# Seven-product feed-forward network of a hybrid backbone: who rounds, who empties PSUM, and in what order TensorE takes its products

## The chip, the cores and the metric

The kernel runs on one core of a Trainium2 chip. The metric is the device time of one execution in microseconds (us). TensorE is called PE here, VectorE DVE, ScalarE ACT, GpSimd POOL, and the queue that issues most transfers SP.

## The reference, cut to what matters

Two layers, each on 1024 latent tokens and 256 context tokens of width 1024. In front of each half of a layer stands a normalisation that is modulated by six vectors, which come from a small input times a large matrix (the "modulations", 1024 x 6144 a layer).

```
m = silu(c) @ w_mod[l] + b_mod[l]          # sh1, sc1, ga1, sh2, sc2, ga2; the same for c_ctx
x = x + ga1 * (mixers(modulate(rms_norm(x), sh1, sc1) @ w_in) @ w_out)
x = x + ga2 * (square(relu(modulate(rms_norm(x), sh2, sc2) @ w_ffn1)) @ w_ffn2)
```

w_ffn1 is 1024 x 4096, w_ffn2 4096 x 1024. The context tokens go through the same with their own modulations, in the last layer only as far as the mixers need them. All is fp32.

## The kernel before, in words

**Products.** An fp32 factor is split in two: a rounded part h (fp32r) and the rest l = x - h. Each product is three matmuls, h·h, h·l and l·h (`mm3`, L141 to L143). So every weight passes one rounding copy and one subtraction on POOL: `split` (L243), in which ACT does the copy (`copy_a`, L130) and POOL the subtraction (L246). `wcols` loads a block of 128 columns of w_ffn1 in two halves of 256 KB through two `raw` buffers (L258); the parts `wh` and `wl` have three buffers each.

**The first layer of the feed-forward network** multiplies the hidden rows (two groups of 512 latent tokens) by w_ffn1 with seven block products instead of eight. The first of the seven, and the whole of the context tokens, are the *first sweep*, `hidden_first` (L1249): for each block `fc` of 128 columns it sums over k = 0 to 7. For the latent rows (even `fc` alone; layer 1 has only these) it copies PSUM after k = 3, while the sum goes on in the same bank:

```
if k == 3 and t0 >= CTX:
    r = self.B()
    self.copy_a(r, ps)
    self.nc.scalar.dma_start(self.part[fc // 2], r)
```

The half sum is kept in HBM (`part`). At the end `squared` (L1243) empties PSUM with a relu, squares and stores, all on ACT. The other six products are the *second sweep*, `hidden_rest` (L1271), in 16 rounds. A round loads a 1024 x 256 block (`weights`, L1283), makes the four sums of its quarters on DVE (L1300 to L1303), rounds five of them on ACT and subtracts on POOL (L1306, L1309), and does the products in `front` and `m5`, `c21`, `c12`, `m7`.

**The quarter** (L1203) makes the other factor's eight combinations for the second sweep from the last group of rows. For four k it has two normalised rows each (a DVE instruction with PSUM, then a bias added by ACT, L133), five DVE additions (L1229 to L1234), and six POOL subtractions (L1230, L1240), five of them each after a rounding copy on ACT.

**Modulations.** A bank (`mod_bank`, L306) multiplies 2048 columns of w_mod by two columns of the input, in 32 columns of PE for each of four groups of PE's columns: 8 steps of k, in each two loads of 512 KB and four fp32 products, two after each load. A product shows as two matmul records. The tiles come from `land`: for the two banks woven into a layer these are the three `e` buffers, for the others `u`.

**Order.** `weave` interleaves generators by their share of a written cost. That gives the priority in which instructions are laid out. The framework's planner then places them on the engines' queues by its own costs, a ready one ahead of one that waits. On the chip each queue is fixed and goes strictly in order. The first sweep is woven with the end of the normalisation and the quarter (`ffn`, L1367); the banks 1 and 2 of the modulations with projections; bank 0 of layer 1 with the last product of layer 0.

Of the kernel before, what the change touches and what calls it, by code (L numbers as in the profile page):

```python
# [13 lines left out]
P = 128  # L14
# [79 lines left out]
class Net:  # L94
# [148 lines left out]
    def split(self, h, l, raw):  # L243

        self.copy_a(h, raw)
        self.nc.gpsimd.tensor_sub(l, raw, f(h))  # L246

# [57 lines left out]
    def mod_bank(self, l, b, land, tag="po"):  # L305
# [3 lines left out]
        for k in range(KD):  # L309
            for hf in range(2):  # L310
# [3 lines left out]
                for q in range(2):  # L314
                    cg = 2 * hf + q
                    nc.tensor.matmul(ps[32 * cg:32 * cg + 32, :], self.csil[:, 2 * k:2 * k + 32], raw[:, 512 * q:512 * q + 512],  # L316
                                     start=k == 0, stop=k == KD - 1, skip_group_check=True,
                                     tile_position=(0, 32 * cg))
                yield 0.9
# [884 lines left out]
    def quarter(self, h, t, x, l, t0, rs):  # L1204
# [12 lines left out]
        def row(k):  # L1217
            a = self.S(n)
            self.stt(a, x.at(k, t0, n), p["s"][1][:, k, 0:1], rb, ALU.mult, ALU.mult)
            self.act(a, a, AF.Identity, bias=p["mods"][:, 24 + k, 0:1])  # L1220
            return a
        for k2 in range(0, 4, 2):
            rows = [(k, row(k), row(k + 4)) for k in (k2, k2 + 1)]
            yield 2.0
            for k, b12, b22 in rows:
# [10 lines left out]
                for raw, r, c, tg in ((t3, t, k + 4, g0), (b22, h, k + 4, g1), (t1, h, k, g1), (t2, t, k, g0),  # L1236
                                      (t4, t, k, g1)):
                    oh, ol = r[0].at(c, tg, n), r[1].at(c, tg, n)
                    self.copy_a(oh, raw)
# [9 lines left out]
    def hidden_first(self, l, h, groups):  # L1249


        hh, hl = h
        w1 = self.I["w_ffn1"][l]
        tags = ("pm", "qk", "qk")
        for fc in range(0, FFN // P, 1 if len(groups) == 3 else 2):
            wh, wl = self.next_weights()[0] if self.wq or self.ready else self.wcols(w1, fc * P)
            for (t0, n) in (groups[:-1] if fc % 2 == 0 else groups[:1]):
                ps = self.PS(self.pick(tags))[:, :n]
                for k in range(KD):
                    c = slice(k * P, k * P + P)  # L1260
                    self.mm3(ps, wh[:, c], wl[:, c], hh.at(k, t0, n), hl.at(k, t0, n), k == 0,
                             k in (3, KD - 1), True)
                    if k % 2:
                        yield n * 2 * 3 * 216e-3 / 512
                    if k == 3 and t0 >= CTX:
                        r = self.B()
                        self.copy_a(r, ps)
                        self.nc.scalar.dma_start(self.part[fc // 2], r)
                self.squared(self.B(n), fc, t0, n, ps)

    def hidden_rest(self, l, h, t):  # L1271
# [11 lines left out]
        def weights(q):  # L1283
            raws = []
            for j in range(2):
# [340 lines left out]
```

## Time and profile before

| | us |
|---|---|
| median of 3 timed runs | 3205.46 (3205.25 to 3210.0) |
| the profiled execution | 3211.08 |
| its span, first to last instruction | 3209.3 |
| busy: PE, DVE, ACT, POOL | 3033.6, 2078.0, 1573.0, 1087.8 |

Times in a row of the profile are counted from the span's start. The first sweep of layer 0 lies at 860 to 1068 us, that of layer 1 at 2484 to 2596; the modulations that are woven in at about 80 to 125, 526 to 606, 1788 to 1843 and 2227 to 2289. Busy time of PE is modelled at its end and overlaps its successor, so a PE that is 95% busy is not at 95% of its peak; what counts is what it waited for.

### The profile page before, as it was taken

Reading aid. Unit: us, or ns where it says so; the run is one execution under the profiler, and the core shown is the slowest. Engines: PE = TensorE matmul, PEld = TensorE weight load, DVE = VectorE, ACT = ScalarE, POOL = GpSimd, SP = SyncE. Lnnn points to the kernel's source line nnn. Section 1 sums busy time; section 2 is a strip of 40 time slices with the busy share of each in tenths; the row PEclk is TensorE's granted clock in tenths of the full one; section 3 lists DMA queues with packets and bytes.
Section 4 is the critical chain, followed back from the end, with each engine's and each line's share of the span. In section 5 each row is a group of like instructions: output and inputs, shape, how many; then the busy total and the mean of one; then the engine's idle time right before and its main releaser. Section 6 shows DMA issues by size and latency. Waiting matters only on the chain.

```text
span 3209.3 us, 46000 instructions
## 1 busy us (share of the span) xinstructions
PE 3033.6 (95%) x16354; PEld 2481.0 (77%) x16354; DVE 2078.0 (65%) x4143; ACT 1573.0 (49%) x3668; POOL 1087.8 (34%) x916
## 2 busy tenths in 40 slices
PE   6998998989978999999999999999999899999998
PEld 4788887778767777888888688787777677777776
DVE  5787777777640344677665777778787544467664
ACT  4575776666454444312111576676675644432111
POOL 2214123232584454222112512223333764522220
PEclk8999999999999999999999999999999999999999
DMA  8300012321334545633222400112322454452221
GB/s 308 93 17 24 22 36 81 128 94 42 130 122 139 177 145 168 221 128 102 86 81 64 153 18 17 27 42 85 116 79 101 147 189 149 158 175 90 95 69 70
DMA packets 239830, 335.97 MB, mean 105 GB/s; under 512 B 37360, under 2 KB 157296, under 8 KB 239600
## 3 DMA queue, kind: packets, MB, share of 16 engines
q1 hardware_dynamic: 211952, 286.88, 28.3%
q10 hardware_dynamic: 27648, 46.15, 3.9%
q8 instruction: 129, 2.11, 0.3%
q14 instruction: 101, 0.83, 0.1%
HBM read 253.28 MB, written 79.69 MB: 104 GB/s over the span
## 4 chain that ended last, share of the span: by engine, by line
PE 50%; POOL 6%; DVE 5%; DMA 4%; ACT 4%; issue 3%; POOLq 0%; ACTq 0%; SPq 0%; DVEq 0%
PE qk L141 6%; PE pm L143 6%; PE qk L143 6%; PE pm L141 5%; PE pm L142 5%; PE qk L142 5%; PE pt L143 3%; PE pt L142 3%; PE pt L141 3%; POOL wl L246 3%; DMA raw<-in_w_ffn 3%; POOL wl L1306 2%; PE pt L743 1%; PE po L316 1%; PE po L752 1%
## 5 line engine op out<-in xcount | busy, mean ns | idle before, releaser
L246 POOL TENSOR_TENSOR wl<-raw,wh 128x512 fp32r<-128x512 f32 (+1 forms) x332 | 459.0, 1395 | 1074.9 <-ACT wh L130 959.2
L130 ACT ACTIVATE wh<-raw 128x512 fp32r<-128x512 f32 (+1 forms) x332 | 203.3, 629 | 791.7 <-PE qk L142 228.2
L141 PE MATMUL pm<-u,wh 128*128 128x512 f32 (+1 forms) x1452 | 540.9, 373 | 9.9 <-ACT b L130 3.2
L143 PE MATMUL pm<-u,wl 128*128 128x512 f32 (+1 forms) x1452 | 534.8, 368 | 8.4 <-POOL wl L246 6.2
L142 PE MATMUL pm<-u,wh 128*128 128x512 f32 (+1 forms) x1452 | 532.6, 367 | 0.0
L141 PE MATMUL qk<-u,wh 128*128 128x512 f32 (+1 forms) x1152 | 433.2, 377 | 33.2 <-ACT b L130 30.8
L143 PE MATMUL qk<-u,wl 128*128 128x512 f32 (+1 forms) x1152 | 433.7, 377 | 5.8 <-POOL wl L246 3.7
L142 PE MATMUL qk<-u,wh 128*128 128x512 f32 (+1 forms) x1088 | 406.6, 374 | 1.9 <-POOL u L434 1.5
L141 PEld LDWEIGHTS pm<-u,wh 128*128 128x128 f32 x1452 | 276.7, 191 | 56.5 <-ACT b L130 5.8
L143 PEld LDWEIGHTS pm<-u,wl 128*128 128x128 f32 x1452 | 275.8, 190 | 52.4 <-POOL wl L246 11.3
L130 ACT ACTIVATE s<-pt 128x512 fp32r<-128x512 f32 (+4 forms) x548 | 251.5, 467 | 120.2 <-PE pt L743 74.0
L142 PEld LDWEIGHTS pm<-u,wh 128*128 128x128 f32 x1452 | 276.6, 191 | 38.1
L136 DVE SCALAR_TENSOR_TENSOR u<-pm,mods,u 128x512 f32<-128x512 f32 (+1 forms) x312 | 216.2, 694 | 110.9 <-PE pm L143 110.3
L141 PEld LDWEIGHTS qk<-u,wh 128*128 128x128 f32 x1152 | 219.4, 190 | 80.7 <-ACT b L130 36.1
L136 DVE SCALAR_TENSOR_TENSOR u<-qk,mods,u 128x512 f32<-128x512 f32 (+1 forms) x296 | 205.7, 695 | 113.1 <-PE qk L143 112.9
L143 PEld LDWEIGHTS qk<-u,wl 128*128 128x128 f32 x1152 | 218.6, 190 | 51.0 <-POOL wl L246 8.3
L1306 POOL TENSOR_TENSOR wl<-u,wh 128x512 fp32r<-128x512 f32 x128 | 185.7, 1475 | 168.5 <-ACT wh L130 168.5
L142 PEld LDWEIGHTS qk<-u,wh 128*128 128x128 f32 x1088 | 206.9, 190 | 41.2 <-POOL u L434 3.5
L133 ACT ACTIVATE b<-b 128x512 f32<-128x512 f32 (+4 forms) x256 | 146.7, 573 | 148.5 <-DVE b L1330 60.3
L133 ACT ACTIVATE e<-qk,t 128x512 f32<-128x512 f32 (+2 forms) x336 | 188.5, 572 | 42.3 <-DVE t L676 27.3
L1300 DVE TENSOR_TENSOR u<-u 128x512 f32<-128x512 f32 x32 | 23.7, 739 | 275.5 <-DMA u<-in_w_ffn 160.8
L747 DVE TENSOR_TENSOR s<-pt,s 128x512 fp32r<-128x512 f32 (+1 forms) x256 | 166.7, 660 | 40.5 <-ACT s L130 36.2
(318 smaller groups left out, 6935.7 us busy)
## 6 DMA issues: line engine op xcount, KB each, us to landing
raw<-in_w_ffn SPq DMA_DIRECT2D x224, 256.0 KB, 2.9
e<-in_w_mod SPq DMA_DIRECT2D x64, 512.0 KB, 4.1
u<-in_w_ffn SPq DMA_DIRECT2D x64, 512.0 KB, 4.6
m<-b ACTq DMA_DIRECT2D x96, 256.0 KB, 3.1
e<-m SPq DMA_DIRECT2D x32, 640.0 KB, 4.7
u<-in_w_mod SPq DMA_DIRECT2D x32, 512.0 KB, 5.5
e<-m SPq DMA_DIRECT2D x32, 512.0 KB, 4.4
xd<-u SPq DMA_DIRECT2D x24, 640.0 KB, 3.4
```

Of the source, the lines that this page charges most:

```text
L130: return self.nc.scalar.activation(o, i, AF.Copy, **k)
L133: self.nc.scalar.activation(o, i, fn, **k)
L136: self.nc.vector.scalar_tensor_tensor(o, a, s, b, op0=op0, op1=op1)
L141: mm(o, ah, bh, start=start, stop=False, skip_group_check=part)
L142: mm(o, ah, bl, start=False, stop=False, skip_group_check=part)
L143: mm(o, al, bh, start=False, stop=stop, skip_group_check=part)
L246: self.nc.gpsimd.tensor_sub(l, raw, f(h))
L316: nc.tensor.matmul(ps[32 * cg:32 * cg + 32, :], self.csil[:, 2 * k:2 * k + 32], raw[:, 512 * q:512 * q + 512], start=k == 0, stop=k == KD ...
L743: nc.tensor.transpose(pt[:, e * 256 + hd * P:e * 256 + hd * P + P], prs[hd][0][:, (i + e) * P:(i + e) * P + P], self.ident)
L747: nc.vector.tensor_sub(tl, pt[:, :w], f(th))
L752: nc.tensor.matmul(po[:, :256], V[:, kc, :], th[:, c], start=i + e == 0, stop=False)
L1306: nc.gpsimd.tensor_sub(lo[i], sr[i], f(hi[i]))
```

## The change

1. `split` copies with DVE while `act_evicts` is set, which `ffn` sets for the woven first sweep. In the quarter the bias additions and the rounding copies go from ACT to DVE. ACT keeps the emptying of PSUM, the squares and the stores.
2. `hidden_first` is cut in parts. In layer 0 an even block does its latent half sum, then the context product in another bank, then the second half. In layer 1 the second half comes after the first half of the next block.
3. In round 0 of the second sweep the weights come as four loads of 256 KB, into two `s` tiles and the two `raw` buffers, and their sums into four `s` tiles, in place of `u` tiles.
4. In each round `m5` comes ahead of the `c21` of the round before.
5. `mod_bank` waits for both loads of a step and does the four products in a row.

```diff
@@ -242,8 +242,14 @@
 
     def split(self, h, l, raw):
 
-        self.copy_a(h, raw)
+        if self.act_evicts:
+            self.nc.vector.tensor_copy(h, raw)
+        else:
+            self.copy_a(h, raw)
         self.nc.gpsimd.tensor_sub(l, raw, f(h))
+
+
+    act_evicts = False
 
     def wsplit(self, loads, n, new=None):
 
@@ -307,16 +313,19 @@
         nc = self.nc
         ps = self.PS(tag)
         for k in range(KD):
+            raws = []
             for hf in range(2):
                 raw = f(land())[:, :1024]
                 c0 = 2048 * b + 1024 * hf
                 nc.sync.dma_start(raw, self.I["w_mod"][l, k * P:(k + 1) * P, c0:c0 + 1024])
-                for q in range(2):
-                    cg = 2 * hf + q
-                    nc.tensor.matmul(ps[32 * cg:32 * cg + 32, :], self.csil[:, 2 * k:2 * k + 32], raw[:, 512 * q:512 * q + 512],
-                                     start=k == 0, stop=k == KD - 1, skip_group_check=True,
-                                     tile_position=(0, 32 * cg))
-                yield 0.9
+                raws.append(raw)
+
+            for cg in range(4):
+                nc.tensor.matmul(ps[32 * cg:32 * cg + 32, :], self.csil[:, 2 * k:2 * k + 32],
+                                 raws[cg // 2][:, 512 * (cg % 2):512 * (cg % 2) + 512],
+                                 start=k == 0, stop=k == KD - 1, skip_group_check=True,
+                                 tile_position=(0, 32 * cg))
+            yield 1.8
         sb = self.B()
         self.copy_a(sb, ps)
         pt = self.PS(tag)
@@ -1217,7 +1226,7 @@
         def row(k):
             a = self.S(n)
             self.stt(a, x.at(k, t0, n), p["s"][1][:, k, 0:1], rb, ALU.mult, ALU.mult)
-            self.act(a, a, AF.Identity, bias=p["mods"][:, 24 + k, 0:1])
+            nc.vector.tensor_scalar(a, a, p["mods"][:, 24 + k, 0:1], None, op0=ALU.add)
             return a
         for k2 in range(0, 4, 2):
             rows = [(k, row(k), row(k + 4)) for k in (k2, k2 + 1)]
@@ -1236,7 +1245,7 @@
                 for raw, r, c, tg in ((t3, t, k + 4, g0), (b22, h, k + 4, g1), (t1, h, k, g1), (t2, t, k, g0),
                                       (t4, t, k, g1)):
                     oh, ol = r[0].at(c, tg, n), r[1].at(c, tg, n)
-                    self.copy_a(oh, raw)
+                    nc.vector.tensor_copy(oh, raw)
                     nc.gpsimd.tensor_sub(ol, raw, f(oh))
                     yield 1.0
 
@@ -1249,24 +1258,50 @@
     def hidden_first(self, l, h, groups):
 
 
+        nc = self.nc
         hh, hl = h
         w1 = self.I["w_ffn1"][l]
         tags = ("pm", "qk", "qk")
+
+        def part(ps, w, t0, n, ks):
+            for k in ks:
+                c = slice(k * P, k * P + P)
+                self.mm3(ps, w[0][:, c], w[1][:, c], hh.at(k, t0, n), hl.at(k, t0, n), k == 0, k in (3, KD - 1), True)
+                if k % 2:
+                    yield n * 2 * 3 * 216e-3 / 512
+
+        def context(fc, w):
+            t0, n = G_CTX
+            ps = self.PS(self.pick(tags))[:, :n]
+            yield from part(ps, w, t0, n, range(KD))
+            self.squared(self.B(n), fc, t0, n, ps)
+
+        def second(fc, w, ps):
+            t0, n = G_LAT[0]
+            yield from part(ps, w, t0, n, range(4, KD))
+            self.squared(self.B(), fc, t0, n, ps)
+        last = None
         for fc in range(0, FFN // P, 1 if len(groups) == 3 else 2):
-            wh, wl = self.next_weights()[0] if self.wq or self.ready else self.wcols(w1, fc * P)
-            for (t0, n) in (groups[:-1] if fc % 2 == 0 else groups[:1]):
-                ps = self.PS(self.pick(tags))[:, :n]
-                for k in range(KD):
-                    c = slice(k * P, k * P + P)
-                    self.mm3(ps, wh[:, c], wl[:, c], hh.at(k, t0, n), hl.at(k, t0, n), k == 0,
-                             k in (3, KD - 1), True)
-                    if k % 2:
-                        yield n * 2 * 3 * 216e-3 / 512
-                    if k == 3 and t0 >= CTX:
-                        r = self.B()
-                        self.copy_a(r, ps)
-                        self.nc.scalar.dma_start(self.part[fc // 2], r)
-                self.squared(self.B(n), fc, t0, n, ps)
+            w = self.next_weights()[0] if self.wq or self.ready else self.wcols(w1, fc * P)
+            if fc % 2 == 0:
+                t0, n = G_LAT[0]
+                ps = self.PS(self.pick(tags))
+                yield from part(ps, w, t0, n, range(4))
+                r = self.B()
+                self.copy_a(r, ps)
+                nc.scalar.dma_start(self.part[fc // 2], r)
+
+                if len(groups) == 3:
+                    yield from context(fc, w)
+                    yield from second(fc, w, ps)
+                else:
+                    if last:
+                        yield from second(*last)
+                    last = fc, w, ps
+            else:
+                yield from context(fc, w)
+        if last:
+            yield from second(*last)
 
     def hidden_rest(self, l, h, t):
 
@@ -1281,18 +1316,28 @@
         NQ = FFN // 256
 
         def weights(q):
-            raws = []
-            for j in range(2):
-                r = self.U()[:, :1024].rearrange("p (k c) -> p k c", k=4)
-                nc.sync.dma_start(r, w1[512 * j:512 * j + 512, 256 * q:256 * q + 256].rearrange("(k p) c -> p k c", p=P))
-                raws.append(r)
+            if q:
+                raws = []
+                for j in range(2):
+                    r = self.U()[:, :1024].rearrange("p (k c) -> p k c", k=4)
+                    nc.sync.dma_start(r, w1[512 * j:512 * j + 512, 256 * q:256 * q + 256].rearrange("(k p) c -> p k c", p=P))
+                    raws.append(r)
+                su = [self.U(), self.U()]
+                sr = [su[i // 2][:, 512 * (i % 2):512 * (i % 2) + 512] for i in range(4)]
+            else:
+
+                raws = {}
+                for i, j in ((0, 1), (1, 1), (0, 0), (1, 0)):
+                    r = (self.S() if j else self.R(512)).rearrange("p (k c) -> p k c", k=4)
+                    nc.sync.dma_start(r, w1[512 * j:512 * j + 512, i * P:i * P + P].rearrange("(k p) c -> p k c", p=P))
+                    raws[i, j] = r
+                sr = [self.S() for _ in range(4)]
 
             def a(i, j):
-                return raws[j][:, :, i * P:i * P + P]
+                return raws[j][:, :, i * P:i * P + P] if q else raws[i, j]
             wl = [self.W()[:, :1024], self.W()[:, :1024]]
             wh = [self.wp.tile([P, 4 * WU], F32R, tag="wh", name="wh", bufs=3)[:, :1024] for _ in range(2)]
-            su = [self.U(), self.U()]
-            lo, hi, sr = ([y[i // 2][:, 512 * (i % 2):512 * (i % 2) + 512] for i in range(4)] for y in (wl, wh, su))
+            lo, hi = ([y[i // 2][:, 512 * (i % 2):512 * (i % 2) + 512] for i in range(4)] for y in (wl, wh))
             lo.append(self.S(n, F32R))
             hi.append(self.S(n, F32R))
             v = [x.rearrange("p (k c) -> p k c", k=4) for x in sr]
@@ -1347,10 +1392,9 @@
         last = None
         for q in range(NQ):
             m5, m7, c21, c12 = front(q)
+            m5()
             if last:
                 last[0]()
-            m5()
-            if last:
                 last[1]()
             m7()
             last = c21, c12
@@ -1364,7 +1408,9 @@
         NF = FFN // P
         self.hid = [self.spill() for _ in range(NF)]
         self.part = [self.dp.tile([P, 512], F32, tag=f"r{l}_{q}", name=f"r{l}_{q}") for q in range(NF // 2)]
+        self.act_evicts = True
         weave((pending, 30), (self.hidden_first(l, h, groups), 90 * len(groups) - 90))
+        self.act_evicts = False
         drain(self.hidden_rest(l, h, t))
         x = self.x = self.unspill_x(x_out, T if len(groups) == 3 else 1024)
 
```

## Rows read from the trace of the kernel before

**Rows 1.** The page, part 1: engine, busy us (share of the span), instructions.

```profile
PE 3033.6 (95%) x16354; PEld 2481.0 (77%) x16354; DVE 2078.0 (65%) x4143; ACT 1573.0 (49%) x3668; POOL 1087.8 (34%) x916
```

**Rows 2.** Windows: stretch, length, busy us (count) by engine, granted clock, DMA.

```profile
core 0: us, PE busy (x) PEld busy (x) DVE busy (x) ACT busy (x) POOL busy (x), PEclk, DMA share, GB/s
895.00:958.00 63.00, 47.05 (x270) 41.07 (x269) 31.34 (x24) 36.35 (x75) 57.10 (x41) 0.92 0.37 113
958.00:1065.00 107.00, 97.25 (x601) 86.45 (x600) 0.00 (x0) 45.55 (x91) 42.26 (x33) 0.98 0.48 146
1065.00:1110.00 45.00, 40.02 (x174) 31.54 (x173) 24.07 (x30) 17.48 (x30) 21.86 (x15) 0.96 0.63 200
2513.00:2584.00 71.00, 64.60 (x269) 49.54 (x269) 33.68 (x26) 45.94 (x83) 64.79 (x46) 1.00 0.50 164
```

**Rows 3.** PE's waits from 860, 895, 958, 1065 (two rows), 2484 (two rows).

```profile
PE qk L141 <- ACT b L130: 3.3, 2, 1.8
...
PE qk L141 <- ACT b L130: 14.3, 4, 5.8
...
PE qk L141 <- ACT b L130: 9.7, 8, 2.0
...
PE pm L141 <- ACT wh L130: 2.4, 1, 2.4
PE pm L143 <- POOL wl L1306: 2.0, 1, 2.0
...
PE qk L141 <- ACT b L130: 3.4, 3, 1.7
PE pm L141 <- ACT b L130: 3.2, 3, 1.3
```

**Rows 4.** Timeline of ACT at 904 to 920: start, length, instruction, [idle before <- releaser].

```profile
915.60 0.63 ACT L130 ACTIVATE wh<-raw 128x512 fp32r<-128x512 f32 x1 [7.86 <-DMA raw<-in_w_ffn]
...
919.01 0.57 ACT L130 ACTIVATE b<-qk 128x512 f32<-128x512 f32 x1
```

**Rows 5.** Timeline of POOL at 899 to 918 and at 556 to 558.

```profile
902.49 1.74 POOL L1240 TENSOR_TENSOR u<-s,u 128x512 fp32r<-128x512 f32 x1
...
905.89 5.14 POOL L1240 TENSOR_TENSOR u<-s,u 128x512 fp32r<-128x512 f32 x3
...
556.20 1.30 POOL L246 TENSOR_TENSOR wl<-raw,wh 128x512 fp32r<-128x512 f32 x1 [3.69 <-ACT wh L130]
```

**Rows 6.** Timeline of PE at 563, 589 to 592, and 1338.

```profile
563.04 1.05 PE L316 MATMUL po<-e,csil 128*32 128x512 f32 x4
...
589.12 1.05 PE L316 MATMUL po<-e,csil 128*32 128x512 f32 x4
...
590.32 0.28 PE L142 MATMUL pm<-wl,u 128*128 128x256 f32 x1
590.44 0.28 PE L143 MATMUL pm<-wh,u 128*128 128x256 f32 x1
...
591.72 1.05 PE L316 MATMUL po<-e,csil 128*32 128x512 f32 x4
...
1338.22 1.07 PE L316 MATMUL po<-u,csil 128*32 128x512 f32 x8
```

**Rows 7.** POOL by line and shape, 958 to 1065: busy us, mean ns, idle before.

```profile
L246 POOL TENSOR_TENSOR wl<-raw,wh 128x512 fp32r<-128x512 f32 x33 | 42.4, 1295 | 61.6 <-ACT wh L130 61.3
```

**Rows 8.** Timeline of DVE at 556 to 558 and at 562.

```profile
556.29 1.50 DVE L1142 TENSOR_SCALAR u<-u 128x512 f32<-128x512 f32 x1
...
562.31 0.42 DVE L1142 TENSOR_SCALAR u<-u 128x512 f32<-128x512 f32 x1
```

**Rows 9.** DMA issues, 526 to 606, then 69 to 125: KB each, median us to landing.

```profile
e<-in_w_mod SPq DMA_DIRECT2D x13, 512.0 KB, 3.9
...
e<-in_w_mod SPq DMA_DIRECT2D x13, 512.0 KB, 4.7
```

**Rows 10.** Timeline of SP's queue at 564.

```profile
564.13 0.34 SPq L313 DMA_DIRECT2D e<-in_w_mod  x1
```

## The prediction, made before the changed kernel was run

> **What bounds the kernel now.** I read the page first: over the whole span TensorE (PE) shows 95% busy, and GpSimd (POOL) 34% [rows 1]. Such means hide the stages, so I cut the span into stretches next [rows 2]. The first sweep of layer 0 runs from about 860 to 1065 us; the "quarter" (the step that makes the eight combinations of the hidden rows) falls into 895 to 958. There PE is busy 47.05 of 63 us and POOL 57.10. After it, to 1065, PE has 97.25 of 107, DVE nothing at all, POOL 42.26. In layer 1 the quarter lies at 2513 to 2584: PE 64.60 and POOL 64.79 of 71. So both quarters run at the pace of POOL, or near it, and the rest of the first sweep does not.
>
> Then I asked what PE waits for in each stretch [rows 3]: almost always a `b` written by ScalarE (ACT), 3.3 + 14.3 + 9.7 us in layer 0 and 3.4 + 3.2 us in layer 1. That `b` is the copy of the half sum after k = 3: PE may not go on in that PSUM bank before ACT has read it. The queues around the longest such wait (5.8 us) show why: ACT stood 7.86 us in front of a rounding `wh<-raw` that waited for its load, and the copy stood behind it, at 919.01 [rows 4]. The load waited for a raw buffer, which POOL freed late, because three subtractions of the quarter (5.14 us) came before the weights' [rows 5]. The copy is ACT's fault; the late load is POOL's.
>
> **Part 1, layer 0 outside the quarter: PE no longer waits for the copy.** After the change the context product stands between the two halves: 24 matmuls of 256 columns, 0.12 us apart [rows 6], 2.9 us, against a copy of about 0.6 us that no rounding now delays. The waits of 860 to 895 and 958 to 1068, 3.3 + 9.7 = 13.0 us [rows 3], go. The granted clock over 958 to 1065 was 0.98 [rows 2], 2.1 us lost after such waits; I count it back: 15 us. Next would be the weights: POOL's two subtractions take 2 x 1.295 us [rows 7] of the 5.7 us that PE needs for one column block (24 x 0.12, and half of 24 at 512 columns, twice as long), and DVE, with nothing to do there, gives two copies. If it has to meet POOL each time (1.50 us, below), two halves take 2 x (1.50 + 1.30) = 5.6 us, just the 5.7. Bounds 8 to 15, since that cover is thin.
>
> **Part 2, roundings on VectorE: the price on POOL.** No copy of SBUF to SBUF by DVE stands in the trace. The nearest row is a tensor_scalar of the same 128x512 fp32: 0.42 us alone, and 1.50 us where it started together with a POOL subtraction of 1.30 us [rows 5, 8]. So a one-input DVE instruction and a POOL instruction do not run side by side. Together they take 1.50 us, so POOL loses at least 0.20 us for each, and at most the 0.42 us. DVE's two-input instructions do the same at a higher price: POOL's 1.295 us [rows 7] becomes 1.74 us in the quarter [rows 5], 0.45 more. A check of this sum: layer 0's quarter has 41 POOL instructions [rows 2] and 20 two-input DVE ones, 41 x 1.295 + 20 x 0.45 = 62.1 us of 63. In layer 1: 46 x 1.295 + 20 x 0.45 = 68.6 of 71. Both quarters are full.
>
> The Trainium skill (SBUF — State Buffer, section "SBUF: two separate sides") calls the port pair that DVE and GpSimd share an exclusive lock held for the whole instruction, for a one-input fp32 DVE instruction in its two-port mode too. By that rule each copy would cost POOL its whole 0.42 us, and the rows bear it out only half: 1.50 is less than 0.42 + 1.30. I take 0.20, the row in which the two met.
>
> In each quarter the change moves 20 copies and 8 bias additions to DVE, and the weights' copies of that time: 17 in layer 0 (41 less the quarter's 24) and 22 in layer 1, so 45 and 50 instructions, 9 and 10 us more for POOL and DVE together.
>
> *Layer 0's quarter.* The waits for `b` (14.3 us) and the clock (0.92 over 63 us, 5 us) could go, 19 us. But the stretch can't become shorter than its POOL work while POOL's order stays: 62 + 9 = 71 us, 8 more than now. If the planner spreads the quarter over the sweep's idle POOL (42.26 of 107 us used), PE gains. Bounds -9 (or -19 at 0.42) to +19; I take +3, nearer to POOL's row than to PE's waits.
>
> *Layer 1's first sweep.* The waits for `b`, 6.6 us, go, since the first half of the next block now stands between. But there is no stretch of idle POOL to spread into: 10 us more on 71, of which the last two blocks after 2584 hide some. Besides, a block's weights are now held until its second half, one half later, with three buffers: the lead for the next ones falls from two blocks to one (5.8 us). Bounds -21 to +6.6; I take -5.
>
> **Part 3, the first weights of the second sweep.** At the border of layer 0 PE waited 2.4 us for `wh` and 2.0 us for `wl` [rows 3], and the clock over 1065 to 1110 was 0.96, 1.8 us. Now four loads of 256 KB (instead of two of 512 KB) go to the two raw buffers and to `s` tiles, which are free after the quarter, not when the hidden rows' `u` tiles are. They are queued on SP behind the sweep's last weight loads, and their DVE additions behind the last copies, in an idle DVE. What stays late is the second `wh` buffer, which the last block but one holds. Bounds 0 to 6; I take 4. In layer 1 the same needs `s` tiles (all eight) that the quarter frees at its end, 2584: nothing is loaded much earlier. Bounds -3 to +4; 1. The order m5 before c21 moves no work out of the second sweep, where PE is not kept waiting; 0.
>
> **Part 4, modulations four in a row.** Now two products of two instructions each stand alone and take 1.05 us; where four products came in a row, they took 1.07 us in all [rows 6]. So a k step costs 1.07 instead of 2.10: 1.03 us less. Four banks of 8 steps are woven with other work: 33 us, if PE is always the bound there. (The first bank of all waits for its loads, and the last bank already runs by eights: 0.)
>
> But a step now needs two of the three `e` buffers at once. One of each step's tiles can load only when the step before is through: the load was issued 1.09 us after the matmuls' start (563.04 and 564.13 [rows 6, 10]) and the median landing is 3.9 us [rows 9], a period of 5.0 us. Today a half step comes every 2.60 us [rows 6], 5.2 per step. If PE stands in order before its load, the gain is 0.2 x 8 x 4 = 6 us, and with the 4.7 us of the first bank [rows 9] it is 0.6 us a step less there: about 0 in all. If the planner puts other projections in between, it is up to 33. Bounds -5 to 33; I take 9, near the ring.
>
> **Sum.** 15 + 3 - 5 + 4 + 1 + 9 = 27 us off the profiled execution's 3211.1 us (span 3209.3). That execution lies 5.6 us above the median of the timed runs, 3205.46, with the same work, so I take the 27 us from the median: **3178 us**.
>
> **Rivals.**
>
> A. *The modulations pay in full.* The planner fills the waits for `e` tiles, so part 4 gives 32 instead of 9. For it: PE waits almost nothing for these loads today, so they are now placed well. Against: the period of 5.0 against 5.2. Time: 27 + 23 = 50 us, 3155.
>
> B. *The change does not do what it says: the waits for `b` turn into waits for `wl`.* PE waits for ACT only because the blocks' weights come at POOL's pace. Then the quarter in layer 0 gives -8 instead of +3, the steady part 8 instead of 15, layer 1 stays at -5: 27 - 18 = 9 us, 3196. For it: POOL's sums of 62 of 63 and 69 of 71 us. Against: after 958 POOL is idle for 61.3 us, waiting for the roundings [rows 7].
>
> C. *Slower: DVE's one-input instructions hold POOL up for their whole length.* Place: both quarters, with POOL's order kept. Price: 0.42 us [rows 8] x 45 = 19 and x 50 = 21 us, and since the `s` tiles of layer 1 come free later, 3 us at its border. The sum is 15 - 19 - 21 + 4 - 3 + 9 = -15: 3220. It decides from 0.26 us an instruction on, where 95 of them take away the other 25 us. (The Trainium skill's lock, on the page named in part 2, is this price.)
>
> **How the numbers follow.** Forecast (15 to 40 us gained) 0.45, A 0.17, B 0.20 (0.08 of it faster, 0.12 within), C 0.18. About 0.2% (6.4 us) is what a measurement of this kernel can tell from no change. Faster 0.45 + 0.17 + 0.08 = 0.70, same 0.12, slower 0.18. The likeliest one's own range is 3165 to 3191. The range for 8 in 10 takes in A with part of part 2's upper bounds (58 us gained) and reaches toward C, up to no gain: 3147 to 3207.
>
> **What would show it.** Part 1: no row of PE waiting for `b` in either first sweep, and 958 to 1065 shorter by some 13 us. Part 2: DVE copies near 0.42 us alone and 1.5 us beside POOL, POOL's mean in the quarters about 0.2 us longer for each, PE's waits now named `wl`; layer 1's first sweep not shorter. Part 3: the wait for `wh` at layer 0's border gone. Part 4: `po` matmuls in runs of eight, 1.0 us each, and, if the ring decides, waits for `e<-in_w_mod` 5 us apart. I am wrong if the quarter of layer 1 is shorter than 71 us, if a step of the modulations comes every 4.2 us, or if the second sweep loses its full PE.

## The result: slower by 1.2%, and the profile after

The changed kernel takes 3247.6 us (median of 4 runs, 3242.77 to 3250.15), the kernel before 3207.36 us beside it (4 runs): a ratio of 1.0123, 95% interval 1.0106 to 1.0141. I had forecast 3178 (3147 to 3207). The profiled execution took 3246.39 us; its span is 3244.6 us, 35.3 more than before (by the medians of the timed runs 40.2 more).

By stages of the two traces, from the stores that ACT issues (a sweep lasts from its first store, or from the last store of the sweep before, to its last one) and from SP's spills of the rows:

| stage | before | after | difference |
|---|---|---|---|
| start to the first sweep of layer 0 | 861.0 | 859.9 | -1.1 |
| layer 0, first sweep | 215.5 | 211.1 | -4.4 |
| layer 0, second sweep | 238.4 | 243.9 | +5.5 |
| layer 0, last product (bank 0 of layer 1 within) | 443.4 | 446.9 | +3.5 |
| from there to the first sweep of layer 1 | 731.3 | 726.2 | -5.1 |
| layer 1, first sweep | 105.8 | 131.7 | +25.9 |
| layer 1, second sweep | 236.0 | 245.3 | +9.3 |
| the rest | 378.1 | 379.6 | +1.5 |

So four places lost, besides 1.5 us at the end, and the largest loss is in the shortest stage. The windows of after that answer to [rows 2]:

```profile
core 0: us, PE busy (x) PEld busy (x) DVE busy (x) ACT busy (x) POOL busy (x), PEclk, DMA share, GB/s
895.00:958.00 63.00, 50.21 (x264) 42.40 (x262) 59.33 (x65) 13.57 (x28) 50.01 (x32) 0.86 0.32 101
958.00:1065.00 107.00, 102.10 (x639) 92.33 (x640) 25.88 (x44) 30.85 (x64) 54.62 (x43) 0.97 0.50 155
1065.00:1110.00 45.00, 45.00 (x207) 37.02 (x206) 25.20 (x34) 19.56 (x34) 26.13 (x19) 1.00 0.65 212
2513.00:2584.00 71.00, 53.96 (x183) 39.30 (x183) 66.27 (x69) 14.54 (x24) 58.12 (x39) 0.84 0.36 115
```

In both quarters DVE is now the full engine (59.33 of 63 us, 66.27 of 71), and POOL does less than before, 32 and 39 instructions against 41 and 46. In layer 1 PE gets 183 matmuls through where it had 269. Outside the quarter, and at layer 0's border, PE gained.

PE's waits of after, answering to [rows 3] (895 to 958, 958 to 1065, and 2484 to 2620; between 1065 and 1110 there is none):

```profile
PE qk L141 <- DVE wh L246: 6.2, 2, 4.5
...
PE pm L141 <- DVE wh L246: 5.7, 1, 5.7
...
PE qk L141 <- ACT b L130: 0.6, 1, 0.6
...
PE pm L141 <- DVE wh L246: 8.2, 2, 4.8
PE qk L143 <- POOL wl L249: 5.1, 4, 1.8
```

The waits for `b` are all but gone, as forecast (0.6 us are left). Waits for weights stand in their place.

The second sweep shows a wait that I had not looked for. From 1110 to 1280 us, first of before, then of after:

```profile
PE qk L141 <- DVE s L1343: 3.2, 11, 0.3
```

```profile
PE qk L141 <- DVE s L1388: 13.1, 8, 1.9
```

This is the product `c21`, which waits for the `u3` of `m7` to leave its PSUM bank. The wait is under 0.3 us a round before and 1.6 us after, and a round takes 15.8 us instead of 14.45. The queues of one round of after, DVE, ACT and POOL (start, length, instruction, [idle before <- releaser]):

```profile
1188.11 0.68 DVE L1388 TENSOR_TENSOR s<-qk,b 128x512 f32<-128x512 f32 x1
1188.82 0.69 DVE L1389 TENSOR_TENSOR s<-pt,s 128x512 f32<-128x512 f32 x1
...
1194.60 0.69 DVE L1345 TENSOR_TENSOR u<-u 128x512 f32<-128x512 f32 x1 [4.49 <-POOL wl L1351]
1195.32 0.69 DVE L1346 TENSOR_TENSOR u<-u 128x512 f32<-128x512 f32 x1
1195.93 0.68 DVE L1375 TENSOR_TENSOR b<-qk,b 128x512 f32<-128x512 f32 x1
...
1201.63 0.69 DVE L1347 TENSOR_TENSOR u<-u 128x512 f32<-128x512 f32 x1 [4.42 <-POOL wl L1351]
1202.24 1.77 DVE L1348 TENSOR_TENSOR u<-u 128x512 f32<-128x512 f32 x1
1203.93 0.68 DVE L1388 TENSOR_TENSOR s<-qk,b 128x512 f32<-128x512 f32 x1
...
1189.54 1.30 ACT L133 ACTIVATE s<-s 128x512 f32<-128x512 f32 x2 [3.67 <-DVE s L1389]
1190.87 0.33 ACTq L1256 DMA_DIRECT2D m<-s  x1
1191.30 1.15 ACT L130 ACTIVATE wh<-u 128x512 fp32r<-128x512 f32 x2 [0.46 <-ACT s L133]
1196.65 1.30 ACT L133 ACTIVATE b<-b 128x512 f32<-128x512 f32 x2 [4.20 <-DVE b L1375]
1197.98 0.33 ACTq L1256 DMA_DIRECT2D m<-b  x1
1198.35 1.15 ACT L130 ACTIVATE wh<-u 128x512 fp32r<-128x512 f32 x2 [0.40 <-ACT b L133]
...
1192.01 2.56 POOL L1351 TENSOR_TENSOR wl<-u,wh 128x512 fp32r<-128x512 f32 x2 [4.38 <-ACT wh L130]
1199.06 2.54 POOL L1351 TENSOR_TENSOR wl<-u,wh 128x512 fp32r<-128x512 f32 x2 [4.50 <-ACT wh L130]
```

Read it in order of time: `u3` on DVE (1188.11), ACT's square (1189.54), the issue of its store, two copies (1191.30), POOL's two subtractions (1192.01), DVE's sums (1194.60) and c21's addition (1195.93), ACT's square (1196.65), the issue, two copies (1198.35), POOL (1199.06), DVE's other sums (1201.63), and `u3` of the next round at 1203.93. The loop closes after 15.82 us. Each step starts within 0.1 us of the end of the one before (POOL's of the first of ACT's two copies), and no PE instruction is in it. `u3` itself could have run some 6 us earlier, when m7 was through (about 1197), but DVE takes it in order, behind L1347, which waits for POOL. So PE ends `m5` at 1203.03 and stands still until 1204.66.

### The profile page after: what moved, and what is told of

The parts are those of the page before. It is cut to its first block, busy times and chain, and to the rows that moved or that the text cites. A ratio compares the mean times of both kernels' runs of the same rounds, so it can differ in the third digit from the quotient of the medians.

```text
span 3244.6 us, 46047 instructions
## 1 busy us (share of the span) xinstructions
PE 3034.6 (94%) x16354; PEld 2493.1 (77%) x16354; DVE 2167.3 (67%) x4291; ACT 1492.1 (46%) x3520; POOL 1084.3 (33%) x916
## 4 chain that ended last, share of the span: by engine, by line
PE 63%; DVE 15%; issue 8%; ACT 6%; POOL 6%; DMA 3%; POOLq 0%; SPq 0%; ACTq 0%; DVEq 0%
PE pm L143 7%; PE pm L141 7%; PE pm L142 7%; PE qk L143 6%; PE qk L141 6%; PE qk L142 6%; PE pt L143 3%; PE pt L142 3%; PE pt L141 3%; DVE u L136 3%; PE pt L752 3%; POOL wl L249 2%; PE po L761 2%; PE po L762 1%; ACT s L130 1%
## 5 line engine op out<-in xcount | busy, mean ns | idle before, releaser
L141 PE MATMUL pm<-u,wh 128*128 128x512 f32 (+1 forms) x1452 | 544.2, 375 | 19.3 <-DVE wh L246 14.9
L130 ACT ACTIVATE wh<-raw 128x512 fp32r<-128x512 f32 (+1 forms) x240 | 145.4, 628 | 669.9 <-PE qk L142 197.7
L143 PEld LDWEIGHTS pm<-u,wl 128*128 128x128 f32 x1452 | 278.3, 192 | 52.5 <-POOL wl L249 13.6
L1351 POOL TENSOR_TENSOR wl<-u,wh 128x512 fp32r<-128x512 f32 x120 | 154.0, 1306 | 240.5 <-ACT wh L130 232.5
L133 ACT ACTIVATE b<-b 128x512 f32<-128x512 f32 (+4 forms) x256 | 146.7, 573 | 139.1 <-DVE b L1375 106.1
L143 PE MATMUL pt<-u,wl 128*128 128x512 f32 (+1 forms) x492 | 186.9, 380 | 3.5 <-POOL wl L249 3.4
```

Of the source, the lines that this page charges most:

```text
L130: return self.nc.scalar.activation(o, i, AF.Copy, **k)
L133: self.nc.scalar.activation(o, i, fn, **k)
L141: mm(o, ah, bh, start=start, stop=False, skip_group_check=part)
L143: mm(o, al, bh, start=False, stop=stop, skip_group_check=part)
L1351: nc.gpsimd.tensor_sub(lo[i], sr[i], f(hi[i]))
```

## The experiments

The stages of all runs, from one profiled execution each (spans and sweeps in us; "POOL" is the time from the first store of layer 1's first sweep to the last subtraction of weights or quarter, and how long POOL was idle in that time, both worked out from its instructions in the trace). The three kernels that leave layer 1's sweeps as they were (before, b_mods, best2) show 341.1 to 341.8 us for both together, so that far one execution repeats another; the stage ahead of layer 0's first sweep takes anything from 854 to 862 us, so that spans say less than sweeps:

| run | span | L0 first | L0 second | L1 first | L1 second | POOL, idle |
|---|---|---|---|---|---|---|
| before | 3209.3 | 215.5 | 238.4 | 105.8 | 236.0 | 94.8, 16.4 |
| after | 3244.6 | 211.1 | 243.9 | 131.7 | 245.3 | 113.5, 28.9 |
| a_m5_back | 3223.2 | 209.9 | 235.6 | 132.6 | 233.8 | 115.8, 31.3 |
| b_m5 | 3226.3 | 213.9 | 252.0 | 104.9 | 247.7 | 94.2, 15.8 |
| a_m5_sp | 3218.3 | 212.5 | 231.4 | 131.4 | 235.2 | 113.4, 28.9 |
| a_l1_act | 3236.8 | 213.0 | 243.8 | 116.2 | 250.7 | 107.0, 28.2 |
| a_l1_nopipe | 3240.6 | 211.8 | 243.8 | 129.2 | 246.3 | 110.4, 25.8 |
| b_split | 3217.9 | 202.1 | 245.3 | 117.9 | 238.7 | 107.0, 28.2 |
| b_split_late | 3211.2 | 201.1 | 244.5 | 113.1 | 240.2 | 101.7, 24.5 |
| b_dve | 3227.1 | 218.3 | 240.1 | 126.1 | 238.9 | 109.9, 25.3 |
| b_wdve | 3212.7 | 209.3 | 239.2 | 117.9 | 237.2 | 103.1, 20.4 |
| b_qdve | 3243.3 | 224.2 | 239.0 | 133.9 | 234.1 | 116.4, 35.5 |
| a_late | 3222.2 | 210.8 | 234.6 | 131.5 | 233.9 | 113.9, 25.6 |
| b_small | 3209.5 | 219.1 | 234.4 | 108.5 | 238.1 | 94.3, 15.9 |
| b_mods | 3207.0 | 216.0 | 239.0 | 104.6 | 236.5 | 93.5, 15.2 |
| best1 | 3207.0 | 210.9 | 236.4 | 110.3 | 238.5 | 96.6, 18.4 |
| best2 | 3189.2 | 202.4 | 234.5 | 106.1 | 235.1 | 95.4, 17.2 |

Names with a_ start from the changed kernel, with b_ from the kernel before.

### The order of m5 and c21

**a_m5_back**

```diff
-            m5()
             if last:
                 last[0]()
+            m5()
+            if last:
                 last[1]()
```

> The changed kernel, with c21 ahead of m5 again in every round. Theory: it is the new place of m5 that stretches a round of the second sweep from 14.45 us (before) to 15.8 us (after), since DVE's u3, for which c21 waits, now stands behind two sums of the weights. Then the ten rounds between the sixth and the last load of a half sum take 141 to 143 us again in both layers (after: 155.5 and 154.0), the 1.6 to 1.8 us waits of the product from s tiles shrink to about 0.3 us, and the whole takes about 3222 us (25 less than after). Rival: the round is longer because the first weights in small tiles and the rounding on DVE have moved ACT's and POOL's queues; then the pitch stays at 15.8 us and the time within 3 us of 3247.

3224.16 us (4 runs; against before 1.0044, 1.0029 to 1.006). The ten rounds take 143.6 and 141.3 us, the wait 2.9 us in ten times. The theory holds (143.6 lies 0.6 above its range).

**b_m5** is the same edit alone, the other way round, on the kernel before.

> The kernel before with m5 ahead of c21 and nothing else. Theory: the ten rounds between the sixth and the last load of a half sum take 153 to 156 us in both layers (before 141.4 and 142.5), the span is 3230 to 3236 us. Rival: the longer round needs another part of the change beside it; then 141 to 146 us and 3207 to 3215 us.

155.1 and 154.0 us, as the theory has it; the span, 3226.3 us, is 17.0 us above the kernel before and below the 3230 to 3236 that I expected. The two second sweeps lose 13.6 + 11.7 = 25.3 us, and the other stages happen to be shorter. PE's waits from 1110 to 1280 are those of after, to the tenth:

```profile
PE qk L141 <- DVE s L1343: 13.1, 8, 1.9
```

**a_m5_sp**

```diff
-        self.nc.scalar.dma_start(self.hid[fc][:, t0:t0 + n], r)
+        (issue or self.nc.scalar).dma_start(self.hid[fc][:, t0:t0 + n], r)
...
-                self.squared(u3, 2 * q + 1, g1, n)
+                self.squared(u3, 2 * q + 1, g1, n, issue=nc.sync)
```

(the same for `r1` and `u2`.)

> The changed kernel, with the stores of the second sweep issued by SP in place of ACT. In after's trace a round of 15.8 us closes as a loop of queues without PE: DVE's sums and c21's addition, ACT's square, the issue of its store (0.33 us, 0.40 to 0.46 us until the next copy), ACT's two copies, POOL's two subtractions, DVE's two other sums and m7's addition, ACT's square, the issue, copies, subtractions, and DVE's sums again. Theory of the loop: without the two issues the round takes 14.9 to 15.1 us. Rival (c21 just stands too near behind m7 on PE): the round stays at 15.7 to 15.9 us.

The span falls to 3218.3 us with m5 still first. SP's loads of a half sum come 14.72 us apart:

```profile
1185.67 0.38 SPq L1367 DMA_DIRECT2D b<-r  x1
...
1200.39 0.37 SPq L1367 DMA_DIRECT2D b<-r  x1
```

That is below the 14.9 to 15.1 that I expected: the two issues had cost more than their own length, and PE is nearly the bound again (its wait is 0.5 us at most). The rival falls: c21 stands no farther behind m7 than in the changed kernel.

### The first sweep of layer 1

**a_l1_act** and **a_l1_nopipe** undo one half each:

```diff
-        self.act_evicts = True
+        self.act_evicts = l == 0
...
-                    nc.vector.tensor_copy(oh, raw)
+                    if l == 0:
+                        nc.vector.tensor_copy(oh, raw)
+                    else:
+                        self.copy_a(oh, raw)
```

```diff
-                else:
-                    if last:
-                        yield from second(*last)
-                    last = fc, w, ps
+                yield from second(fc, w, ps)
```

(the bias additions of the first go back to ACT in the same way; in the second the line stands for both layers.)

> The changed kernel, but in layer 1 the copies of the weights and of the quarter and the bias additions are on ACT, as before; the order of the halves in the first sweep stays as changed. Theory: the 26 us that the first sweep of layer 1 lost (105.8 to 131.7 us) come from DVE, which is busy without a gap from 2520 to 2560 us, because its instructions take 1.5 to 1.8 us beside POOL where they take 0.4 to 0.7 us alone. Then the sweep takes 100 to 106 us and the whole about 3221 us. Rival: the sweep is longer because the second half of a sum now comes a block later, which holds a PSUM bank and the weights' buffers longer; then the sweep stays above 120 us and the whole above 3236 us.

> The changed kernel, but in layer 1 the second half of a sum follows its first half at once, as before; the roundings stay on DVE. DVE theory: the first sweep of layer 1 stays at 126 to 134 us and the whole within 4 us of 3247. Rival (the late second half holds banks and weights): the sweep falls to 105 to 112 us and the whole to 3222 to 3228 us.

With ACT's roundings the sweep takes 116.2 us: 15.5 of the 26 come back, not all, and 5.4 are lost again behind it (3237.63 us, 1.0083). So neither theory had the first run. With the old order and DVE's roundings it takes 129.2 (3243.0 us, 1.0103), where the theory of DVE had put it. The roundings on DVE cost more here than the late second half, but neither is the whole.

**b_split**, **b_dve**, **b_wdve** and **b_qdve** do one part alone on the kernel before, with the lines of the diff as they stand: the new `hidden_first` (point 2 of the change); all of point 1; of point 1 the copies of the weights; and the copies and biases of the quarter. The last is

```diff
-            self.act(a, a, AF.Identity, bias=p["mods"][:, 24 + k, 0:1])
+            nc.vector.tensor_scalar(a, a, p["mods"][:, 24 + k, 0:1], None, op0=ALU.add)
...
-                    self.copy_a(oh, raw)
+                    nc.vector.tensor_copy(oh, raw)
```

> The kernel before, with the new order of the first sweep alone (context between the halves in layer 0, the second half a block later in layer 1); all copies stay on ACT. Theory: the waits for b go by this order alone, and layer 0's first sweep takes 209 to 212 us (before 215.5); in layer 1 the sweep is held up by weights that are needed earlier, 112 to 118 us (before 105.8). Rival, by my forecast of 15 us: layer 0's sweep takes 200 us. Second rival: with the roundings still on ACT the order gains nothing in layer 0, 214 to 217 us.

> The kernel before, with the roundings and the bias additions of the first sweep on DVE in both layers and nothing else. Theory: DVE has room for them in layer 0, where the quarter lies beside more products, 213 to 217 us (before 215.5), and not in layer 1, 127 to 133 us (before 105.8), with DVE busy over 65 of the 70 us from 2510 us on. Rival: the loss in layer 1 needs the new order of the halves too; then its sweep takes 106 to 115 us.

> The kernel before, with the copies of the weights alone on DVE in the first sweeps; the quarter's copies and biases stay on ACT. Capacity theory: DVE is busy 35.5 of the 70 us from 2510 us on; some 18 to 21 copies of about 1.0 us bring it to 53 to 57, which fits, and layer 1's first sweep takes 103 to 110 us (before 105.8). Rival (the order in DVE's queue): copies that wait for their raw tile hold up the quarter, or stand behind it; then the sweep takes over 115 us with DVE idle for more than 10 us of the 70.

> The kernel before, with the quarter's copies and bias additions alone on DVE; the copies of the weights stay on ACT. Capacity theory: 20 copies of 1.26 us and 8 additions of 0.85 us are 32 us beside DVE's 35.5, 67 of 70: DVE is just filled, and layer 1's first sweep takes 108 to 118 us, between the kernel before (105.8) and both moves (126.1). Rival (any rounding on DVE beside POOL costs as much as the whole): over 122 us.

Layer 1's two sweeps together take 341.8 us before, and 356.6, 365.0, 355.1 and 368.0 here: every part costs by itself, and the quarter on DVE alone as much as the whole change without m5 (366.4). My theory of DVE's capacity falls: in b_wdve DVE is busy 42.61 us of the 70 from 2510 on, and the sweep is still 12 us longer. (In layer 0 I was off too: 202.1 us in b_split where I expected 209 to 212, 218.3 in b_dve where I expected up to 217.)

What the runs share stands in the last column of the table: POOL is done 7 to 22 us later. In order of POOL's end (before and the seven runs that change layer 1's first sweep and have c21 ahead of m5: 94.8, 101.7, 103.1, 107.0, 109.9, 113.9, 115.8, 116.4) the two sweeps take 341.8, 353.3, 355.1, 356.6, 365.0, 365.4, 366.4 and 368.0 us. POOL has the same 56 to 58 instructions in that time in all of them; their mean is 1.43 us before and 1.48 after, and POOL is idle for 20 to 36 us instead of 16.4.

POOL's waits up to that end, of before and of after:

```profile
POOL wl L246 <- ACT wh L130: 5.9, 8, 1.1
POOL s L1230 <- ACT s L133: 3.9, 1, 3.9
```

```profile
POOL wl L249 <- DVE wh L246: 11.6, 12, 2.2
POOL u L1249 <- DVE u L1248: 5.3, 11, 1.7
POOL s L1239 <- DVE s L1229: 3.6, 1, 3.6
```

And of b_split:

```profile
POOL wl L246 <- ACT wh L130: 20.0, 9, 3.8
```

A subtraction can't start before its copy, so it is tempting to call these waits the cause. But most of the waiting for the weights' copies lies behind the quarter's last subtraction (2578.6 in after, 2559.9 in b_split). For after, the same wait up to 2579, and then the window behind it (its first busy time is PE's):

```profile
POOL wl L249 <- DVE wh L246: 1.7, 4, 0.6
...
2580.00:2602.00 22.00, 21.99 (x88) 17.68 (x89) 4.45 (x8) 6.10 (x10) 11.59 (x9) 0.92 0.60 185
```

For b_split, from 2561 to its end, and the window:

```profile
POOL wl L246 <- ACT wh L130: 17.6, 5, 3.8
...
2562.00:2590.00 28.00, 26.17 (x109) 19.57 (x108) 0.00 (x0) 11.91 (x22) 12.48 (x10) 1.00 0.50 163
```

There PE is busy 21.99 of 22 and 26.17 of 28 us, and waits 1.8 and 1.9 us: POOL waits, and PE hardly does. In b_split ACT stands about 3.5 us a block for PE's half sum, empties and squares, and only then makes the two roundings that POOL waits for. So this waiting follows PE's pace and does not explain the loss. The loss is made before. When the quarter's last subtraction is through, all 32 of the weights' subtractions are done in the kernel before, 22 in after and in b_split, 24 in b_dve and b_wdve, 20 in b_qdve. Up to there POOL is idle for 16.4 us before and 19.0 in after, 10.6 in b_split, 17.5 in b_qdve.

**a_late** and **b_split_late** ask whether it is merely the order: in the changed kernel ten of the weights' subtractions stand behind the quarter's last one in POOL's queue, before none.

```diff
-        weave((pending, 30), (self.hidden_first(l, h, groups), 90 * len(groups) - 90))
+        weave((pending, 30 if l == 0 else 12), (self.hidden_first(l, h, groups), 90 * len(groups) - 90))
```

> The changed kernel with c21 ahead of m5 again, and in layer 1 the quarter's share in the first sweep's order cut from 30 to 12, so that 2 of the weights' subtractions stand behind the quarter's last one in POOL's queue instead of 10 (before: none). Both sweeps of layer 1 together take 341.8 us before and 366.4 us with c21 back. Theory of the order (the sweep is late by the weights that were laid out behind the quarter, some 2.8 us of PE each): they take 345 to 354 us together, the span is 3203 to 3211 us. Rival (DVE has too much to do, in whatever order): what the first sweep gains, the second loses as a wait for the quarter, 360 to 368 us together, the span 3217 to 3225 us.

> The kernel before with the new order of the first sweep alone (as the earlier run), and in layer 1 the quarter's share cut from 30 to 12: 4 of the weights' subtractions stand behind the quarter's last one in POOL's queue instead of 10. Both sweeps of layer 1 together took 356.6 us with the order alone (before 341.8). Theory of the order: 344 to 351 us. Rival (the late second half holds a bank and the weights' buffers, which costs wherever the weights stand): 354 to 358 us.

a_late gains nothing: 365.4 us for both sweeps, as its rival has it, though the weights went ahead. b_split_late gains 3.3 us of 14.8, between the two. So the place in POOL's queue is not the cause with DVE's roundings (in a_late POOL waits for copies of weights instead, 14.4 us before the quarter's end), and at most a part of it without. What holds the weights back is open: DVE's instructions, which are slowed by POOL (the rows are below, under the hardware), their order on DVE, or the two raw tiles. No run here has a third raw tile, which would ask that.

### The small first weights and the modulations

**b_small** (the new `weights`, point 3) and **b_mods** (the new `mod_bank`, point 5), each alone on the kernel before.

> The kernel before, with the small tiles for the first weights of the second sweep and nothing else. Theory: the start of layer 0's second sweep owes its 7 to 9 us to this (first to sixth load of a half sum 56 to 59 us, before 65.4); the sweep takes 234 to 237 us (before 238.4), layer 1's 234 to 237 us (before 236.0). Rival: the start was shorter because the first sweep left other buffers free; then 64 to 66 us and 238 us.

> The kernel before, with the four products of a modulation step in a row and nothing else. After's trace has the last store ahead of the first sweeps 0.6 us earlier in layer 0, and layer 1 from its start to its first sweep 3.5 us shorter, but the end of layer 0's last product 3.6 us later, where bank 0 of layer 1 now runs in 92 us instead of 205 us. Theory: the two cancel, 3204 to 3209 us, with the stretch from the end of the second sweep of layer 0 to the end of its last product 3 to 4 us longer. Rival, as I forecast: 9 us are gained, 3198 us, and the 3.6 us in layer 0 are of another part of the change.

The small weights alone move nothing in layer 0 (453.5 us for both sweeps, before 453.9) and cost 4.8 us in layer 1 (its second sweep takes 238.1 us, above the 234 to 237 that I expected), though POOL is done there as early as before. With `b_split` in place they pay: there PE waited 4.7 us for the first `wh` at layer 0's border, and in best2 this wait is gone. The modulations alone: 3211.97 against 3210.02 us (11 and 15 runs), 1.0007, 0.9996 to 1.0017, no change; both medians lie above the 3204 to 3209 that I expected, and the 9 us of the rival are not there. The two banks of layer 1 gain 5.5 us, and the last product of layer 0 loses 4.0. There a pair of blocks used to carry one step of bank 0 and now carries two, so the later pairs carry none and wait for weights. From 1315 to 1760, of before and of b_mods:

```profile
PE qk L143 <- POOL wl L246: 2.0, 3, 0.9
PE pm L143 <- POOL wl L246: 1.9, 2, 0.9
PE pt L143 <- POOL wl L246: 1.2, 2, 0.6
```

```profile
PE qk L143 <- POOL wl L246: 3.4, 4, 0.9
PE pt L143 <- POOL wl L246: 3.1, 4, 0.9
PE pm L143 <- POOL wl L246: 2.4, 3, 0.9
```

### Versions that keep what gained

**best1**: a_m5_back, a_l1_act and a_l1_nopipe together, with one `next(mg, None)` a pair of blocks instead of two. **best2**: the kernel before with the new `hidden_first` in layer 0 (layer 1 in the old order), the small first weights in layer 0 alone (`if q or l:` in place of `if q:`), the new `mod_bank`, and one `next(mg, None)`.

```diff
-            if q:
+            if q or l:
...
             next(mg, None)
-            next(mg, None)
```

> The changed kernel with what lost undone: c21 ahead of m5 again, the first sweep of layer 1 in its old order with its roundings and bias additions on ACT, and bank 0 of layer 1's modulations with one step a pair of blocks as before; layer 0's first sweep, the small first weights and four products in a row stay. If the parts add up as the profiles have them (layer 0's first sweep 5.6 us shorter, its second 2.8, layer 1 from its start to its first sweep 3.7, the setup 0.8), the profiled span is 3196 us (3193 to 3200) and the first sweep of layer 1 takes 104 to 107 us. Rival: the first sweep of layer 1 lost its 26 us through something that these edits don't reach (the small first weights take its s tiles and raw buffers); then it stays above 110 us and the whole above 3201 us.

> The kernel before with three parts alone: in layer 0 the context product between the two halves (layer 1 as before) and the small first weights, and the four products of a modulation step in a row, with bank 0 of layer 1 at one step a pair of blocks. All roundings stay on ACT, c21 stays ahead of m5. If the parts add up (the order alone took 13.4 us from layer 0's first sweep and gave 7 back in the second, where PE waited 4.7 us for the first weights, which the small tiles avoid; the modulations 4 to 5 us in layer 1), the span is 3209 - 13 + 0 to 2 - 4.5 = 3190 to 3195 us, and the two sweeps of layer 0 together take 438 to 443 us (before 453.9). Rival: what the first sweep saves only comes back as a wait for the quarter's last rows, whatever the weights do; then the two sweeps take 447 us and the whole 3198 to 3203 us, no better than the version with DVE's roundings in layer 0.

best1 takes 3202.5 us (6 runs; 0.9971 of before, 0.9958 to 0.9983), less than expected from its parts, and as the rival had it: its small weights still cost layer 1 some 7 us. best2 takes 3190.27 us (5 runs) against 3212.2: 0.9928, 0.9914 to 0.9942. It is faster than both kernels; layer 0's two sweeps take 436.9 us (before 453.9), a little better than the 438 to 443 expected.

## Why the prediction was wrong

**The step that failed first** is "The order m5 before c21 moves no work out of the second sweep, where PE is not kept waiting; 0." It cost 21 us of the 35 (a_m5_back against after), 25 in the second sweeps where it stands alone (b_m5). I looked at PE, which waited for next to nothing, and did not ask what the other queues would do. Moving one product made the planner lay out the queues of DVE, ACT and POOL anew, into a loop of 15.82 us without PE, longer than the 14.45 us that a round had taken. a_m5_sp bears the loop out: with its two issues taken away the round falls to 14.72 us. I had named a second sweep that loses its full PE as what would prove me wrong, and priced it at nothing.

**Part 2, layer 1: -5 forecast, -26 measured** (-24.6 over both sweeps with c21 back; below my bound of -21). I took POOL's busy time as what grows, by 0.20 us for each of 50 DVE instructions, and the length of the quarter as what counts. Both were off. Up to the quarter's end POOL's mean rose by 0.08 us (1.43 to 1.51), some 4 us in all instead of 10, and the quarter became shorter (from its first subtraction to its last 70.8 us before, 64.9 after). What I had no term for is which subtractions pass POOL by then: 22 of the weights' 32, where all 32 had. The experiments show that the roundings on DVE and the late second half each cost 13 to 26 us over both sweeps by themselves (b_wdve, b_qdve, b_split); by which queue they do it stays open. Rival C had the sign and the place. Its price, 0.42 us an instruction or 21 us, is not in POOL's busy time either. The row from which I took the price had it already: POOL's subtraction took 1.30 us there, as it does alone, and DVE's instruction 1.50 instead of 0.42 [rows 5, 8].

**Part 2, layer 0's quarter: +3 forecast.** DVE's roundings cost 2.8 us alone (b_dve) and 7.8 us beside the new order (202.1 in b_split, 209.9 in a_m5_back). The copies of the weights gain there (209.3 in b_wdve), those of the quarter lose more (224.2 in b_qdve).

**Part 1: right.** 13.4 us by itself in layer 0's first sweep (b_split), against 15, and where I had put it: 13.0 of them lie between the 24th store of that sweep's squares, some 112 us from its start in both kernels, and the last. (In the quarter ahead of it, waits for `b` remain while ACT rounds, 8.1 us in b_split, before 14.3.) Half of the 13.4 came back as a wait at the border until the small weights were there, which is the use that part 3 has (+4 forecast for layer 0). In layer 1, where I had +1 for the small weights, they cost 5.

**Part 4: +9 forecast; 5.5 gained and 4.0 lost.** The step's cost is as read, 1.07 us for eight records, where they stand in a row. But the planner still takes many steps apart: in after's trace 15 of the 32 steps stand in a row, in the first bank one of eight. I had counted all 32. That bank 0 would run at twice its pace, since a `yield` now stands for a whole step, was in the diff, and I passed over it.

Of the sum of 27 us, only part 1 was worth what I gave it, and DVE's roundings in layer 0's quarter took more than half of it back.

## What to carry to other kernels

Before you cost an edit of order at nothing, follow one round through every in-order queue and add up the loop that closes without the busiest engine: here one product's new place made it 15.82 us where a round had taken 14.45. Before you call an engine's waiting the cause, look where it lies: of POOL's 11.6 us of waiting for `wh` in after, 9.9 lie where PE is busy throughout. Try the parts one by one: of this change one part in one layer, with two helpers, was worth 0.7%, and the rest cost 2%.

## What the hardware showed that I had not expected

A one-input copy on DVE pays most of the price of meeting POOL, and POOL little. DVE and then POOL, after, in layer 1's quarter:

```profile
2526.64 1.51 DVE L246 CAST wh<-raw 128x512 fp32r<-128x512 f32 x1
2528.07 1.51 DVE L1248 CAST u<-s 128x512 fp32r<-128x512 f32 x1
...
2534.61 0.41 DVE L246 CAST wh<-raw 128x512 fp32r<-128x512 f32 x1
...
2526.13 1.74 POOL L1249 TENSOR_TENSOR u<-s,u 128x512 fp32r<-128x512 f32 x1
2527.82 1.48 POOL L1239 TENSOR_TENSOR s<-s 128x512 f32<-128x512 f32 x1
```

A copy takes 0.41 us where it starts while POOL is idle and 1.51 us beside a subtraction; over 2510 to 2580 us the quarter's 18 copies from `s` to `u` average 1.26 us. POOL's subtraction takes 1.30 us where DVE runs nothing (19 of them in before, 2510 to 2580) and 1.44 us in the mean of the seven in after that met copies alone. The Trainium skill (SBUF — State Buffer, section "SBUF: two separate sides") says that whichever of the two starts first has the shared port pair for its whole instruction and the other is blocked. The trace agrees with that for DVE as the one that is blocked. I had read the rule as a price on POOL; by the rows it is mostly one on DVE, 0.85 us for a copy in the mean (1.26 less 0.41) against 0.14 for POOL.

PE's granted clock fell with its waits, to 0.84 from 2513 to 2584 us (1.00 before [rows 2]), a mixture of its two levels, 1.2 and 2.4 GHz. In that stretch a matmul's busy time is 53.96 / 183 = 0.295 us, before 64.60 / 269 = 0.240.
